# Attention loop: each output block unbroken in TensorE's queue, and the last token block's exponentials scaled in their own slot

## The chip, the cores and the metric

The kernel runs on one core of a Trainium2 chip. A core has TensorE (PE, with its weight loads, PEld), which multiplies matrices into the accumulation banks (PSUM); VectorE (DVE), ScalarE (ACT) and GpSimd (POOL), which work on elements; and SyncE (SP), from which most transfers are issued. Each engine takes its own instructions strictly in the order in which they stand in its queue, and waits at the head of the queue when an operand isn't there. The metric is the device time of one execution in microseconds (us), the median of several. For the kernel before it is 1900.26 us, over three runs from 1899.99 to 1901.23.

## The reference

Two layers of a decoder over 512 tokens of 1024 features, everything in float32. Each layer is a half-step feed-forward network, a token mixer and another half-step feed-forward network. The first mixer is a gated short convolution, the second an attention with three branches, of which the change touches two. Cut to what matters here:

```python
q = rms_norm(q) # 16 heads in 4 groups, 64 features each
s_w = q @ k_win.T * scale + rel_bias[distance]     # window branch: here every earlier token
p_w = masked_softmax(s_w, valid_w); o_w = p_w @ v_win
s_s = q @ k_sel.T * scale + rel_bias[distance]     # selected branch: here all blocks are selected
p_s = masked_softmax(s_s, valid_s); o_s = p_s @ v_sel
o_c = softmax over 31 compressed keys, times v_cmp
out = gate0 * o_c + gate1 * o_s + gate2 * o_w
return out @ w_out
```

With 512 tokens, a window of 512 and 8 blocks of which 16 may be chosen, both large branches are plain causal attention over all tokens, with different keys and values.

## The kernel before, in words

All sub-layers run one after the other, and most of the time goes to the large matrix products, which are computed with each float32 operand split in a high and a low part (`mm3`, lines 168 to 171: three matmuls each). The change lies in `attend` (from line 1200), the loop of the attention.

**Units and slots.** A unit is one head with one of the two key branches: 4 groups x 4 heads x 2 branches = 32 units. Two heads of a pair follow each other with the same branch, so units 2n and 2n + 1 share an output. The loop at line 1398 runs over slots v and is a pipeline by hand: in slot v, the scores of unit a = v + 3 are made, the exponentials of unit a - 1 are scaled, unit b = v + 1 is transposed, and in odd slots the outputs of units v - 1 and v are multiplied. Each slot has three thirds, c = 0, 1, 2, which deal with different blocks of 128 tokens: `(3,)`, then `(2, 0)`, then `(1,)` for the scores.

What each helper issues:

- `logits` (line 1271): on TensorE, two matmuls for each token block i, of the queries against the first (i + 1) x 128 keys, high and low part; 8 in a unit. The result `s` lies in one of two banks, s0 and s1, in turn.
- `smallest` (1286): on VectorE, adds the bias table, writes `L` to SBUF and keeps the smallest value of each row in `st`. This is what empties a score bank. `L` has three buffers.
- `exponentials` (1296): on ScalarE, the exponential of `L` in place, with the row's sum in `st`.
- `scaled` (1303): a reciprocal `r` of the four sums on VectorE, the factor `f` (reciprocal times gate) on GpSimd, and four in-place scalings of `L` by `f` on GpSimd, rows 0 to 3, the last of them 512 wide. It stands in the first third of the slot after the one that made the exponentials.
- `turn` (1313): ten transposes `pt` of 128 x 128 on TensorE (4, 4 and 2 in the thirds), each of which needs its row scaled, then copies `p` to SBUF, by ScalarE and (the second third) by VectorE. `pt` has three banks.
- `apply` (1329): the output block. For a pair of heads, eight float32 matmuls into one bank `o`, whose weights are 64 wide: the even head writes the lower 64 partitions, the odd head the upper 64, one after the other. The profile shows two records for each of these, so a block has 16. With the second branch two more pairs for the compressed keys follow (20 records), and the block is finished and split into `ohi` and `olo`.
- `fill` (1402): what is put in between: the query and value projections for later groups (`nat`), the output projection of finished groups (`y`), the compressed branch (`pc`, `pct`), and the turning of the next group's heads and keys (`pk`, `turned`, then moves by DMA into `q` and `k`). `nat`, `y`, `pc` and `pk` share two banks.

At each change of group, around slots 3 to 5, 11 to 13 and 19 to 21, the next group's queries and keys are normed, transposed and moved. The first scores of the new group (unit 8, 16 or 24) need them.

**What sets the order.** The order of each engine's queue is fixed when the kernel is compiled. A scheduler takes instructions in the order in which they are traced, but lets a later one go ahead when, by its estimate of the times, an earlier one isn't ready. `tc.issue_after(ins)` adds an edge for what is traced within it: on the engine of `ins`, and only there, these instructions stand behind `ins`. It adds an order in the queue, no wait. Before the change there are two such edges: `apply` stands behind the last transpose traced so far (line 1416), and the filler of the last third behind the last matmul of `apply` (line 1424). All else may fall in between the matmuls of a block, and in five of the 16 blocks it does.

## Time and profile before

| | us |
|---|---|
| median of three runs | 1900.26 |
| the profiled execution's own time | 1900.41 |
| its span, first to last instruction | 1898.6 |
| TensorE busy over the span | 1871.1 |
| VectorE busy | 1561.7 |
| ScalarE busy | 855.5 |
| GpSimd busy | 226.4 |
| stage of the attention loop | 1325 to 1533 |

Outside the span lie 1.8 us of the profiled execution. Busy time of TensorE runs from the start of a matmul to its modelled end, so that one which could overlap the next but doesn't counts as busy too; what a piece of the queue really takes is read from the starts of the instructions, or from the busy time of one tile in a window. In the views of instructions in order of time, the first number is the start in us from the span's start, the second the length, then engine, line, operation, tiles written and read, the shape, and how many are merged in the row; a number in brackets is the idle time of the engine before, with what ended it. The granted TensorE clock is 1.000 throughout.

### The profile page before, as it was taken

The page shows a single profiled execution, that of the slowest core. Times are in us where ns is not written, and L with a number is a line of the kernel's source. Part 1 is how long each engine was busy: PE and PEld are TensorE (multiplying, and loading weights), DVE is VectorE, ACT ScalarE, POOL GpSimd, SP SyncE. Part 2 cuts the span into 40 slices and gives each one's busy share as a digit, 9 for nine tenths or more (in the row PEclk, how much of TensorE's full clock was granted, in tenths as well). Part 3 has the DMA queues.
Part 4 walks back from the last instruction along what each step waited for, and adds up shares of the span by engine and source line. Part 5 has one row for each costly group of instructions (what it writes and reads, how often), then busy time and mean ns, then how long its engine had stood idle before and what let it go on. Part 6 is the DMA issues. An engine that isn't in the chain of part 4 may idle for free.

```text
span 1898.6 us, 33944 instructions
## 1 busy us (share of the span) xinstructions
PE 1871.1 (99%) x13293; PEld 1710.1 (90%) x13293; DVE 1561.7 (82%) x2671; ACT 855.5 (45%) x1399; POOL 226.4 (12%) x330
## 2 busy tenths in 40 slices
PE   6999999999999999999999999999999999999999
PEld 4989999988899899999989899999777789898989
DVE  8978888887898888888888888887778778586865
ACT  3434344532245343435634343463667636353432
POOL 0011110000011111100111110000444410010100
PEclk9999999999999999999999999999999999999999
DMA  9587767366756767664667766234333235464731
GB/s 327 177 255 191 242 181 230 116 229 233 249 156 183 233 177 239 184 218 117 172 222 189 225 176 203 82 114 127 96 90 84 70 86 160 133 189 124 187 110 64
DMA packets 126669, 324.60 MB, mean 171 GB/s; under 512 B 16011, under 2 KB 16651, under 8 KB 126508
## 3 DMA queue, kind: packets, MB, share of 16 engines
q1 hardware_dynamic: 95196, 242.72, 38.1%
q0 software_dynamic: 31312, 79.71, 18.4%
q8 instruction: 104, 1.70, 0.4%
q14 instruction: 57, 0.47, 0.1%
HBM read 313.85 MB, written 3.15 MB: 167 GB/s over the span
## 4 chain that ended last, share of the span: by engine, by line
PE 84%; DVE 8%; issue 3%; ACT 2%; POOL 1%; DMA 1%; DVEq 0%; SPq 0%; ACTq 0%; POOLq 0%
PE gu L171 13%; PE gu L169 13%; PE gu L170 13%; PE y L169 7%; PE y L170 7%; PE y L171 7%; PE cv L169 2%; PE cv L170 2%; PE cv L171 2%; PE hs L170 2%; PE hs L169 2%; PE hs L171 2%; PE ty L170 1%; PE ty L171 1%; PE o L1340 1%
## 5 line engine op out<-in xcount | busy, mean ns | idle before, releaser
L165 ACT ACTIVATE whi<-wraw 128x1024 fp32r<-128x1024 f32 (+2 forms) x261 | 254.4, 978 | 372.7 <-PE y L170 193.4
L166 DVE TENSOR_TENSOR wlo<-wraw,whi 128x1024 fp32r<-128x1024 f32 (+2 forms) x261 | 294.4, 1133 | 24.4 <-ACT whi L165 23.4
L169 PE MATMUL y<-ahi,whi 128*128 128x512 f32 x576 | 223.7, 391 | 1.0
L170 PE MATMUL y<-alo,whi 128*128 128x512 f32 x576 | 224.3, 389 | 0.0
L171 PE MATMUL y<-ahi,wlo 128*128 128x512 f32 x576 | 224.1, 389 | 0.0
L149 DVE CUSTOM_DVE_ANT_0 adaraw<-adaraw,cond,adabs 128x1024 f32<-128x1024 f32 x144 | 185.8, 1307 | 31.3 <-DMA adaraw<-in_adaw 31.0
L169 PE MATMUL gu<-hhi,whi 128*128 128x256 f32 x696 | 192.5, 277 | 0.0
L171 PE MATMUL gu<-hhi,wlo 128*128 128x256 f32 x696 | 192.4, 276 | 0.0
L170 PE MATMUL gu<-hlo,whi 128*128 128x256 f32 x696 | 192.4, 276 | 0.0
L657 POOL DMA_DIRECT2D qa<-in_ffi x70 | 84.4, 1206 | 712.9 <-DMA qa<-in_ffi 169.4
L169 PE MATMUL gu<-th,qah 128*128 128x256 f32 x584 | 161.3, 276 | 0.0
L170 PE MATMUL gu<-tl,qah 128*128 128x256 f32 x584 | 161.2, 276 | 0.0
L171 PE MATMUL gu<-th,qal 128*128 128x256 f32 x584 | 161.2, 276 | 0.0
L169 PE MATMUL gu<-th,qbh 128*128 128x256 f32 x584 | 161.2, 276 | 0.0
L170 PE MATMUL gu<-tl,qbh 128*128 128x256 f32 x584 | 161.2, 276 | 0.0
L171 PE MATMUL gu<-th,qbl 128*128 128x256 f32 x584 | 161.2, 276 | 0.0
L169 PEld LDWEIGHTS y<-ahi,whi 128*128 128x128 f32 x576 | 107.3, 188 | 27.0 <-ACT ahi L165 5.7
L169 PEld LDWEIGHTS gu<-hhi,whi 128*128 128x128 f32 x696 | 130.7, 188 | 0.5
L170 PEld LDWEIGHTS gu<-hlo,whi 128*128 128x128 f32 x696 | 130.6, 188 | 0.5
L171 PEld LDWEIGHTS gu<-hhi,wlo 128*128 128x128 f32 x696 | 130.7, 188 | 0.0
L171 PEld LDWEIGHTS y<-ahi,wlo 128*128 128x128 f32 x576 | 108.2, 188 | 22.6
L170 PEld LDWEIGHTS y<-alo,whi 128*128 128x128 f32 x576 | 108.1, 188 | 22.1
(312 smaller groups left out, 5379.8 us busy)
## 6 DMA issues: line engine op xcount, KB each, us to landing
wraw<-in_ffi SPq DMA_DIRECT2D x103, 512.0 KB
adaraw<-in_adaw POOLq DMA_DIRECT2D x79, 512.0 KB, 4.9
qa<-in_ffi SPq DMA_DIRECT2D x146, 256.0 KB
wraw<-in_ffo SPq DMA_DIRECT2D x96, 384.0 KB
qa<-in_ffi POOLq DMA_DIRECT2D x70, 512.0 KB, 6.8
adaraw<-in_adaw SPq DMA_DIRECT2D x65, 512.0 KB
a<-in_ffi SPq DMA_DIRECT2D x73, 256.0 KB
wraw<-in_cwi SPq DMA_DIRECT2D x24, 512.0 KB
```

The source lines that it names most:

```text
L149: return nc.vector.tensor_tensor_reduce(out=raw, in0=raw, in1=cond, scale=scale, scalar=adabs[:, c:c + 1], op0=ALU.mult, op1=ALU.add, accu ...
L165: act = nc.scalar.activation(hi, src, AF.Copy)
L166: return act, nc.vector.tensor_tensor(lo, src, hi, ALU.subtract)
L169: nc.tensor.matmul(o, sh, mh, start=first, stop=False)
L170: nc.tensor.matmul(o, sh, ml, start=False, stop=False)
L171: nc.tensor.matmul(o, sl, mh, start=False, stop=last)
L657: nc.gpsimd.dma_start(qa, bass.AP(tensor=a21.tensor, offset=a21.offset, ap=[a21.ap[0], [0, 2], a21.ap[1]]), accum_op=ALU.add)
L1340: last = nc.tensor.matmul(o[half[e], j * P:T], vn[b][j][:, g], both[e][0][:, cc:cc + n], start=(b == 0 and j == 0), stop=False)
```

## The change

Three things change in the loop. `scaled` takes the rows to work on: rows 0, 1 and 2 are scaled where all four were, and row 3 (the last 128 tokens), whose exponentials are made in the first third of a slot, in the last third of that same slot, so that each unit has two reciprocals and two factors, of three rows and of one. `apply` is traced within `behind_all`: an edge to each of the last 40 TensorE instructions among the last 200 instructions traced, in place of the one to the last transpose. And `logits`, `turn` and `fill` are, in every third, traced within `behind_block`, an edge to the last matmul of the newest `apply`.

```diff
-            def scaled(u):
+            def scaled(u, rows):
                 g, q, b = units[u]
+                m = slice(rows[0], rows[-1] + 1)
                 r = sp.tile([P, NB], F32, name="r")
-                nc.vector.reciprocal(r, sts[u][:, NB:2 * NB])
+                nc.vector.reciprocal(r[:, m], sts[u][:, NB + m.start:NB + m.stop])
                 f = sp.tile([P, NB], F32, name="f")
-                nc.gpsimd.tensor_tensor(f, r, gsb[:, :, (g * 4 + q) * 3 + 2 - b], ALU.mult)
-                for i in range(NB):
+                nc.gpsimd.tensor_tensor(f[:, m], r[:, m], gsb[:, m, (g * 4 + q) * 3 + 2 - b], ALU.mult)
+                for i in rows:
                     l = Ls[u][:, LOFF[i]:LOFF[i] + (i + 1) * P]
                     nc.gpsimd.tensor_scalar(l, l, f[:, i:i + 1], 0.0, op0=ALU.mult, op1=ALU.add)
...
+            @contextmanager
+            def behind_all(engine):
+                with ExitStack() as es:
+                    for i in [i for i in nc.cur_bb.bb.instructions[-200:] if i.engine == engine][-40:]:
+                        es.enter_context(tc.issue_after(i))
+                    yield
+
+            def behind_block():
+                return tc.issue_after(last_out[0].ins) if last_out else nullcontext()
+
...
                 for c in range(3):
                     if 0 <= a < N:
-                        sps = logits(a, c)
+                        with behind_block():
+                            sps = logits(a, c)
                     if c == 0 and 0 <= a - 1 < N:
-                        scaled(a - 1)
+                        scaled(a - 1, (0, 1, 2))
+                    if c == 2 and 0 <= a < N:
+                        scaled(a, (3,))
                     if 0 <= b < N:
-                        low = turn(b, c)
+                        with behind_block():
+                            low = turn(b, c)
                     if u % 2 and 0 < u and c == 2:
-                        with tc.issue_after(last_turn[0].ins):
+                        with behind_all(last_turn[0].ins.engine):
                             last_out[:] = [apply(u - 1)]
...
-                    with tc.issue_after(last_out[0].ins) if last_out and c == 2 else nullcontext():
+                    with behind_block():
                         fill(c)
```

## The prediction

> **What bounds the kernel now.** I read the page first, then the busy time of the engines over the attention stage, then that of single tiles and the instructions in order of time around the blocks that the change touches.

> ```profile
> span 1898.6 us, 33944 instructions
> PE 1871.1 (99%) x13293; PEld 1710.1 (90%) x13293; DVE 1561.7 (82%) x2671; ACT 855.5 (45%) x1399; POOL 226.4 (12%) x330
> ```
> ```profile
> 1325.00:1533.00 208.00, 203.23 (x1370) 155.75 (x1369) 160.36 (x480) 133.63 (x369) 82.05 (x160) 1.00 0.30 82
> ```

> TensorE (PE) is busy for 99% of the span, and for 203.23 of the 208 us from 1325 to 1533, which hold the loop that is changed (the columns are PE, weight loads, VectorE, ScalarE, GpSimd, then TensorE's granted clock). So TensorE's queue sets the time, what it saves or loses in this stage reaches the end almost whole (the stages behind it are matmuls again), and no engine but VectorE, 77% busy here, comes near. But a busy TensorE is not one that does its work at the best price. The output blocks show that. `apply` makes 16 of them, one for each odd slot v from 1 to 31: 16 matmul records for the first key branch, 20 for the second. Eleven stand in one piece. Of the windows below, all for tile `o` on TensorE, the first five hold the blocks that stand in pieces (slots 3, 5, 13, 21, 23), the last two a whole block of each size.

> ```profile
> 1355.70:1361.90 6.20, 4.23 (x20) 1.00 0.33 128
> 1369.20:1375.02 5.82, 3.80 (x16) 1.00 0.50 117
> 1417.80:1424.29 6.49, 3.59 (x16) 1.00 0.46 105
> 1468.00:1475.51 7.51, 3.58 (x16) 1.00 0.44 105
> 1484.10:1489.70 5.60, 4.01 (x20) 1.00 0.22 89
> 1398.80:1401.20 2.40, 2.32 (x16) 1.00 0.45 106
> 1386.20:1389.40 3.20, 3.17 (x20) 1.00 0.04 10
> ```

> A matmul of the block fills half of the array's columns (its weights are 64 wide), and its partner the other half. Held together, the two halves run side by side; where the queue is cut between partners, each runs alone.

> **The change, part by part.** *Whole blocks.* The five split ones cost 4.23 - 3.17 = 1.06, 3.80 - 2.32 = 1.48, 1.27, 1.26 and 4.01 - 3.17 = 0.84 us too much: 5.9 us in all. That is the most that holding them together can save, give or take a tenth of a microsecond at each of the ten cuts. It isn't all won, since the pieces now fill time in which TensorE would otherwise stand. Slot 5, in order:

> ```profile
> 1368.48 0.82 PE L1320 MATMUL pt<-ident,L 128*128 128x128 f32 x6
> 1369.23 1.07 PE L1340 MATMUL o<-p,vn 128*64 128x512 f32 x2
> 1370.23 0.66 PE L1166 MATMUL pk<-ident,qn 128*128 128x128 f32 x4
> 1371.82 1.25 PE L1281 MATMUL s<-k,q 128*128 128x512 f32 x6
> 1374.01 0.50 PE L1281 MATMUL s<-k,q 128*128 128x256 f32 x2
> 1375.02 0.38 PE L169 MATMUL nat<-whi,hhi 128*128 128x256 f32 x1
> ```
> ```profile
> 1368.80 0.76 DVE L1184 SCALAR_TENSOR_TENSOR k<-pk,kgs,turned 64x512 fp32r<-64x512 f32 x1
> 1370.68 1.21 DVE L166 TENSOR_TENSOR wlo<-wraw,whi 128x1024 fp32r<-128x1024 f32 x1
> 1371.93 0.74 DVE L1193 SCALAR_TENSOR_TENSOR q<-pk,qgs,turned 64x512 fp32r<-64x512 f32 x1
> 1372.87 0.69 DVE L1291 CUSTOM_DVE_ANT_0 L<-s,tb 128x512 f32<-128x512 f32 x1 [0.19 <-POOL L L1311]
> ```

> With `behind_all` the block goes behind everything of its slot: the turned heads (pk) and all three sets of scores (s). pk needs the bank that VectorE empties with `k`, until 1368.80 + 0.76 = 1369.56, so TensorE stands 0.3 us from 1369.23. The six score matmuls follow at about 1370.1 if the moved keys have landed (they have by 1371.82; no view tells how much sooner). The last two scores need one of two score banks back, which VectorE empties with the first `L`. Ahead of that in its queue is `wlo`, to 1371.89; then L takes 0.69, to 1372.6. Those scores (0.50 at 1374.01) and the block, 2.32, end at 1375.4, against 1375.02 now. If `q` stays ahead of L too, it is 1376.1; if L goes first, 1374.4. I take 0.2 lost, between 1.1 lost and 0.6 won.

> ```profile
> 1417.81 1.07 PE L1340 MATMUL o<-p,vn 128*64 128x512 f32 x2
> 1419.40 1.07 PE L1340 MATMUL o<-p,vn 128*64 128x512 f32 x4
> 1420.40 0.68 PE L1281 MATMUL s<-k,q 128*128 128x512 f32 x2
> 1422.41 0.50 PE L1281 MATMUL s<-k,q 128*128 128x256 f32 x2 [0.30 <-DVE st L1291]
> 1424.29 0.38 PE L169 MATMUL nat<-whi,hhi 128*128 128x256 f32 x1
> 1470.68 1.33 DVE L166 TENSOR_TENSOR ehlo<-wraw,ehhi 128x1024 fp32r<-128x1024 f32 x1
> ```

> Slot 13 has the same shape without a `wlo` in the way. Without the two pieces ahead of them (1.07 us each) the first scores start 1.5 to 2 us before 1420.40, at 1418.7; the last come 2.0 us later (1422.41 - 1420.40, bound by VectorE, as the 0.30 shows), and with 0.50 and 2.32 the block ends at 1423.5: 0.8 won, between 0.3 and 1.1. Slot 21 is as slot 5, with `ehlo` (1.33) in `wlo`'s place, but has six matmuls of the output projection for a filler: 0.3 won, between 0.6 lost and 0.8 won.

> ```profile
> 1357.66 0.69 DVE L1291 CUSTOM_DVE_ANT_0 L<-s,tb 128x512 f32<-128x512 f32 x1
> 1361.90 0.50 PE L1281 MATMUL s<-k,q 128*128 128x512 f32 x1
> ```

> Slot 3 is bound by the score banks. As VectorE's queue stands, its last scores can't go before the L that ends at 1357.66 + 0.69 = 1358.35; with 0.50 for them and 3.17 for the block that makes 1362.0, where the next scores stand now (1361.90): nothing, within half a microsecond.

> ```profile
> 1484.17 1.72 PE L1340 MATMUL o<-p,vn 128*64 128x512 f32 x6
> 1485.82 0.50 PE L169 MATMUL y<-ohi,whi 128*128 128x512 f32 x1
> 1487.40 0.97 PE L1340 MATMUL o<-p,vn 128*64 128x384 f32 x7
> 1489.70 0.50 PE L169 MATMUL y<-ohi,whi 128*128 128x512 f32 x1
> 1485.14 0.27 DVE L1242 TENSOR_TENSOR lc<-pc,lc 128x120 f32<-128x120 f32 x1
> ```

> In slot 23 the six y between the pieces are traced a slot earlier (the share of `out_steps(1)` puts them in slot 22), so the block must go behind them, and they wait for a bank that VectorE empties with `lc`, until 1485.41. y from 1485.5 (1.58 us, 1485.82 to 1487.40), then 3.17: 1490.3, which is 0.6 lost; if VectorE takes `lc` sooner, up to 0.84 won. I take 0.3 lost, nearer the row as it stands.

> Sum: -0.2 + 0.8 + 0.3 + 0 - 0.3 = 0.6 us won; by the ends, from 2.5 lost to 3.8 won. The eleven whole blocks and `behind_block` on the first two thirds of a slot order nothing that isn't so ordered now. Behind a waiting block stand the next slot's scores, transposes and fillers, and for them ScalarE and VectorE; only TensorE's instructions get the edge, so weights are fetched as before.

> *The last tokens' row sooner.*

> ```profile
> L1306 DVE RECIPROCAL r<-st 128x4 f32<-128x4 f32 x32 | 5.5, 172 | 4.6 <-ACT L L1300 4.3
> L1308 POOL TENSOR_TENSOR f<-r,gsb 128x4 f32<-128x4 f32 x32 | 8.6, 267 | 123.8 <-DVE r L1306 100.7 <-ACT p L1326 10.3 <-PE pt L1320 7.5
> L1311 POOL TENSOR_SCALAR L<-L,f 128x512 f32<-128x512 f32 x32 | 24.7, 773 | 0.0
> ```
> ```profile
> PEld pt L1320 <- POOL L L1311: 1.5, 4, 0.5
> PE pt L1320 <- POOL L L1311: 0.7, 2, 0.3
> ```
> ```profile
> 1364.11 2.05 POOL L1311 TENSOR_SCALAR L<-L,f 128x128 f32<-128x128 f32 x4
> 1370.42 3.05 POOL L1311 TENSOR_SCALAR L<-L,f 128x128 f32<-128x128 f32 x4
> ```

> The 512-wide scaling, 0.77 us of GpSimd, leaves the end of the chain exponentials, reciprocal, factor, scaling, transposes. TensorE waits on that chain for at most 1.5 + 0.7 = 2.2 us in the whole stage, so 2.2 is the most it gains, less what is next late. Added are 32 reciprocals (32 x 0.172 = 5.5 us of VectorE) and 32 factors (32 x 0.267 = 8.5 us of GpSimd). GpSimd, 82 of 208 us busy, hides its own. VectorE has 48 us free, but hardly any around the three changes of group (slots 3 to 5 and their like), where each extra reciprocal of two or three units delays the L on which the scores wait: up to 3 x 3 x 0.172 = 1.5 us lost. The new reciprocal waits for exponentials made two thirds of a slot earlier, so what is queued behind it on VectorE (smallest, the copy of p) seldom stands. I take 0.5 won, between 1.5 lost and 2.2 won. The two GpSimd rows are the same four scalings and factors of the same unit kind, once 2.05 and once 3.05 us; in the second VectorE's `wlo` (1370.68, 1.21 us, two SBUF inputs) ran beside it. [...]

> Both parts: 0.6 + 0.5 = 1.1 us won. The profiled run took 1900.41 us, 0.15 above the median of the three, 1900.26, so the forecast is 1899.3 there and 1899.2 for the median; by the ends (4.0 lost, 6.0 won) 1894.3 to 1904.3. A measurement of this kernel can tell about 0.2%, 3.8 us, from no change.

> **The rivals.** *The whole saving lands.* The stage's order is computed when the kernel is compiled, and with the pieces gone it may put L ahead of `wlo`, `q` and `lc`. Then the holes close and 5.9 of the blocks and a little of the scaling arrive: 1900.3 - 6.3 = 1894.0. For it: VectorE's 48 free us, and at 1420.40 nothing but order holds the scores. Against it: the rows of slots 3 and 5, where VectorE works without a break.

> *The score banks turn over too slowly.* Two banks hold the scores, and each waits for VectorE's L. Now pieces of the block run while it does so; afterwards nothing may. If at each change of group the keys arrive only at 1371.82 and L stays where it is, at 1372.87, the last scores of slot 5 go at 1373.6 (1372.87 + 0.69) and the block ends 0.50 + 2.32 later, at 1376.4: 1.4 lost, three times, and 0.6 in slot 23. That is 4.8 lost: 1905.1. It decides once a change of group loses more than about 1.1 us.

> *The edges don't hold the blocks.* `behind_all` takes the last 40 of TensorE's instructions among the last 200 traced; what is older could still fall in between, and the time stays at 1900 within a microsecond. The y of slot 23, the oldest that I know, stands only 22 back on TensorE by the code (a slot makes 8 score matmuls and 10 transposes, and y falls after the second third), so this is unlikely.

> **How the numbers follow.** Forecast 0.50, whole saving 0.27, slow banks 0.18, blocks not held 0.05. By itself the likeliest case spans 1896 to 1903. Faster by over 0.2% (under 1896.5): the whole saving and a tail of the forecast, 0.30. Slower by over 0.2% (over 1904.1): the slow banks, 0.18. Within: 0.52. The range, 1893.0 to 1905.2, takes in the two rivals about their centres and leaves a tenth at each end.

> **What would show it.** Tile `o` should take 2.32 or 3.17 us in each of 16 unbroken blocks, so that the five windows lose 5.9 us together. If the forecast holds, most of that comes back as TensorE waiting for VectorE's `st`, `k` or `lc` just before slots 3, 5, 21 and 23. r and f should count 64 each, and the 2.2 us of waiting for GpSimd fall below 1. I am wrong if the stage from 1325 to the last block shrinks by over 4 us, or grows; and if the time moves outside this stage.

## The result, and the profile after

The kernel after takes 1924.36 us (median of 4 runs, 1923.69 to 1926.27); the kernel before, run beside it, 1900.74 us (1899.99 to 1902.09). The ratio is 1.0128, 95% interval 1.0113 to 1.0143: 24 us slower, 19 us beyond the upper end of the range, and on the side that had the smallest chance.

From the page of the kernel after, the span, the busy time of the engines and the granted clock in 40 slices:

```profile
span 1921.9 us, 34093 instructions
...
PE 1875.0 (98%) x13293; PEld 1713.5 (89%) x13293; DVE 1566.3 (81%) x2703; ACT 858.2 (45%) x1399; POOL 234.2 (12%) x362
...
PE   7999999999999999999999999999788999999999
...
PEclk9999999999999999999999999999899999999999
```

The span grew by 23.3 us (1921.9 - 1898.6). TensorE does the same 13293 matmuls and is only 3.9 us busier, so most of the time is idle. And the slices show where: the 29th to the 31st (48.05 us each, so 1345 to 1490 us) have 7, 8 and 8 tenths of TensorE, and the first of them a granted clock of 8 tenths, where the page of before has a 9 in all of these. In the shares of the whole span, 99% against 98%, 23 us hardly show.

The windows of the output blocks, tile `o` on TensorE in the kernel after (length, busy time and records, granted clock, DMA share, GB/s):

```profile
1353.90:1357.80 3.90, 3.64 (x16) 0.66 0.82 334
1369.80:1375.00 5.20, 5.06 (x20) 0.63 0.36 76
1424.80:1429.80 5.00, 4.87 (x20) 0.66 0.37 79
1481.40:1487.20 5.80, 5.56 (x20) 0.58 0.29 65
1384.00:1387.00 3.00, 2.37 (x16) 1.00 0.35 79
1397.00:1401.00 4.00, 3.23 (x20) 1.00 0.02 4
```

All 16 blocks now stand in one piece, as the change wants, and twelve take 2.37 or 3.23 us in this view (the last two rows). The other four, those of slots 1, 3, 11 and 19, have a granted clock of about 0.6 beside them and take 1.27 + 1.83 + 1.64 + 2.33 = 7.1 us more than the short ones. Three of them (slots 1, 11 and 19) were whole before, and cost nothing then.

The chain of waits on TensorE from 1325 to 1560, after (total us, times, longest), and the same view of before:

```profile
PE pk L1166 <- DVE qn L960: 14.5, 3, 5.6
PE pct L1262 <- DVE pcs L1257: 6.7, 1, 6.7
PE s L1281 <- DVE st L1291: 2.8, 4, 1.2
```
```profile
PE s L1281 <- DVE st L1291: 1.7, 5, 0.5
PE pt L1320 <- POOL L L1311: 0.7, 2, 0.3
PE pk L1166 <- DVE qn L960: 0.6, 2, 0.4
```

Four waits make 21.2 us: one for the compressed probabilities `pcs`, ahead of their transposes `pct`, and three for the normed heads `qn`, ahead of their transposes `pk`. Before, the two together cost 0.6. In order of time around slot 3, before and then after:

```profile
1359.19 0.48 PE L1281 MATMUL s<-k,q 128*128 128x256 f32 x2
1359.61 0.97 PE L1340 MATMUL o<-p,vn 128*64 128x384 f32 x7
...
1360.79 1.19 PE L1345 MATMUL o<-pcp,vz 128*64 128x512 f32 x3
...
1362.48 0.60 PE L1320 MATMUL pt<-ident,L 128*128 128x128 f32 x4
1362.91 0.38 PE L1166 MATMUL pk<-ident,kn 128*128 128x128 f32 x2
1363.13 0.38 PE L1166 MATMUL pk<-ident,qn 128*128 128x128 f32 x2
```
```profile
1363.85 0.38 PE L1321 MATMUL pt<-ident,L 128*128 128x128 f32 x2
1368.67 1.29 PE L1166 MATMUL pk<-ident,qn 128*128 128x128 f32 x4 [4.45 <-DVE qn L960]
1369.90 4.20 PE L1341 MATMUL o<-p,vn 128*64 128x512 f32 x16
1373.93 1.02 PE L1346 MATMUL o<-pcp,vz 128*64 128x512 f32 x4
1374.89 0.74 PE L1281 MATMUL s<-k,q 128*128 128x512 f32 x2
```

Before, the block and the next scores go first, and the first pk that reads `qn` follows 3.5 us after the slot's last scores (1363.13 against 1359.19 + 0.48 = 1359.67), without a wait. After, this pk goes first. VectorE makes `qn` no sooner: from the reduction of `vq` to the end of `qn` it takes 8.9 us (from 1360.31), against 8.5 before (from 1354.51). So TensorE stands for 4.45 us (such a stretch is called a hole below); behind pk stands the block, whose operands were turned in earlier slots, and behind the block all of the next slot. The row of VectorE that makes `qn` before, then VectorE in the hole, after:

```profile
1361.75 1.29 DVE L960 TENSOR_TENSOR qn<-qn,rs_r 128x512 f32<-128x512 f32 x2
```

```profile
1363.44 1.22 DVE L166 TENSOR_TENSOR wlo<-wraw,whi 128x1024 fp32r<-128x1024 f32 x1
...
1366.18 0.47 DVE L216 TENSOR_TENSOR rs_a<-rs_r 128x16 f32<-128x16 f32 x1
...
1367.34 0.56 DVE L220 SCALAR_TENSOR_TENSOR rs_r<-rs_a,rs_r 128x16 f32<-128x16 f32 x1
1367.93 1.29 DVE L960 TENSOR_TENSOR qn<-qn,rs_r 128x512 f32<-128x512 f32 x2
```

It works its way through the inverse square root of the norms, small steps between scores and copies, and reaches `qn` at 1367.93.

The same instructions that follow a hole are slow. Four pk records take 1.29 us here; the prediction's row of before has 0.66 for four. The clock over this stretch, after (the columns of the engines as in the prediction):

```profile
1366.80:1373.60 6.80, 4.92 (x18) 2.25 (x20) 3.94 (x11) 1.29 (x3) 2.48 (x6) 0.50 0.37 102
1364.00:1366.70 2.70, 0.23 (x3) 0.00 (x0) 2.70 (x13) 2.62 (x10) 1.62 (x4) 1.00 0.35 79
```

The granted clock is 1.00 for the first 2.6 us of the hole (which starts at 1364.22) and 0.50 for the 6.8 us after that, well into the block. The holes of slots 1, 11 and 19 show the same: one spell at 0.50 each, of 6.8 us, begun 3.5, 2.2 and 4.8 us into the hole. The clock is 1.00 in every other block. The trace shows no one length of standing as the condition: the spells begin 2.2 to 4.8 us into holes of 4.45 to 6.72 us, and the two holes of 4.45 us (slots 3 and 11) differ in it by 0.4 us. Their beginnings are 1349.74, 1366.80, 1421.42 and 1479.44, worked out from the mean clock of 0.69, 0.52, 0.58 and 0.72 in the windows of 0.1 us from 1349.70, 1366.80, 1421.40 and 1479.40: the later three lie 17.06, 71.68 and 129.70 us behind the first. To within 0.1 us that is 5, 21 and 38 times half a spell (6.83 / 2; the one of slot 3 ends at 1373.63, by 0.84 in the window from 1373.60). So the length of a hole doesn't by itself tell when its spell begins.

So the sum: 21.2 us of waits, less 0.6 of before; 7.1 us in the four blocks; pct (1.09 us for four in the order of time, against 0.66) and three sets of pk (1.29 each, against 0.66) 2.3 more; less the 5.9 us of the split blocks that are whole now: 24.1, against 23.3 of the span.

### The profile page after: what moved, and what is told of

It reads as the page before. It is cut to its first block, busy times and chain, and to the rows that moved or that the text cites. A ratio compares the mean times of both kernels' runs of the same rounds, so it can differ in the third digit from the quotient of the medians.

```text
span 1921.9 us, 34093 instructions
## 1 busy us (share of the span) xinstructions
PE 1875.0 (98%) x13293; PEld 1713.5 (89%) x13293; DVE 1566.3 (81%) x2703; ACT 858.2 (45%) x1399; POOL 234.2 (12%) x362
## 4 chain that ended last, share of the span: by engine, by line
PE 89%; DVE 7%; ACT 2%; issue 1%; DMA 1%; DVEq 0%; SPq 0%; ACTq 0%
PE gu L171 13%; PE gu L169 13%; PE gu L170 13%; PE y L169 7%; PE y L171 7%; PE y L170 7%; PE o L1341 2%; PE cv L169 2%; PE cv L170 2%; PE cv L171 2%; PE hs L170 2%; PE hs L169 2%; PE hs L171 2%; PE ty L170 2%; PE ty L171 2%; PE ty L169 2%
## 5 line engine op out<-in xcount | busy, mean ns | idle before, releaser
L166 DVE TENSOR_TENSOR wlo<-wraw,whi 128x1024 fp32r<-128x1024 f32 (+2 forms) x261 | 293.8, 1131 | 24.0 <-ACT whi L165 22.8
L169 PE MATMUL y<-ahi,whi 128*128 128x512 f32 x576 | 223.7, 392 | 1.0
L169 PE MATMUL gu<-hhi,whi 128*128 128x256 f32 x696 | 192.5, 277 | 0.0
L169 PE MATMUL gu<-th,qah 128*128 128x256 f32 x584 | 161.4, 276 | 0.0
L169 PE MATMUL gu<-th,qbh 128*128 128x256 f32 x584 | 161.2, 276 | 0.0
L169 PEld LDWEIGHTS y<-ahi,whi 128*128 128x128 f32 x576 | 107.3, 188 | 26.9 <-ACT ahi L165 5.6
L169 PEld LDWEIGHTS gu<-hhi,whi 128*128 128x128 f32 x696 | 130.6, 188 | 0.5
```

Source lines behind the costliest of these rows:

```text
L166: return act, nc.vector.tensor_tensor(lo, src, hi, ALU.subtract)
L169: nc.tensor.matmul(o, sh, mh, start=first, stop=False)
```

## The experiments

The theory: `pct` (slot 0's last third) and the first half of the next group's heads, `pk` (the second third of slots 3, 11 and 19), are traced ahead of the blocks of slots 1, 3, 11 and 19, and they wait for VectorE. `behind_all` puts the block behind them; `behind_block` puts everything later behind the block. Together the edges leave nothing that TensorE may do in the wait, and a long wait (4.45 us and more in this kernel) is followed by half the clock (0.50). The rivals: the scaled row delays VectorE; one edge alone costs the time; whole blocks cost it; or the score banks do.

**The scaled part alone** (before, with only this, and `scaled` taking rows as in the change):

```diff
-                        scaled(a - 1)
+                        scaled(a - 1, (0, 1, 2))
+                    if c == 2 and 0 <= a < N:
+                        scaled(a, (3,))
```

> The kernel before with the split of the scaling alone (row 3 in its own slot, rows 0 to 2 a slot later); no new edges in TensorE's queue. Theory (the block is queued behind fillers that wait for VectorE): no hole, 1900.7 us within 3. Rival A (the extra reciprocals and factors delay the chain of exponentials): most of the 24 us is here, 1912 us or more, with TensorE waiting for GpSimd or for L. Rival B (what is held behind the block starves VectorE and ScalarE): 1900.7 within 3.

1900.06 us, ratio 0.9999 (0.9990 to 1.0008). It does nothing, to within 2 us. The whole loss lies with the edges.

**`behind_all` alone** (before, with only this):

```diff
-                        with tc.issue_after(last_turn[0].ins):
+                        with behind_all(last_turn[0].ins.engine):
```

> The kernel before with one edit: the output block stands behind the last 40 TensorE instructions. All four rows are scaled together, and nothing new is held behind the block. Theory: four holes of 4 to 7 us, before pct in slot 1 and before pk in slots 3, 11 and 19, each followed by some 7 us at half clock: 1918 to 1928 us. Rival A: 1900 within 4. Rival B: 1900 within 4, since scores and transposes may go on during a hole.

1902.99 us, ratio 1.0015 (1.0005 to 1.0024). This missed: I had put the whole loss on this edge, and it is 3 us. TensorE's waits and the block of slot 3:

```profile
PE pk L1166 <- DVE qn L960: 5.9, 5, 3.5
```
```profile
1365.14 1.04 PE L1166 MATMUL pk<-ident,qn 128*128 128x128 f32 x6 [3.48 <-DVE qn L960]
1366.11 4.04 PE L1341 MATMUL o<-p,vn 128*64 128x512 f32 x16
```

All blocks are whole and stand behind pct and pk, as in the kernel after. But the next slot's scores and transposes aren't tied to the block, and go ahead of it while pct and pk wait: 5.9 us of waiting for `qn` instead of 14.5, and none for `pcs` in this view. Where the wait is still 3.48 us, the block behind it takes 4.85 us (1366.11 to the next matmul at 1370.96), at a granted clock of 0.67 from 1365.80 to 1371.00. The block of slot 11 is slow too: it runs from 1417.20 to 1422.12, 4.92 us, at a lower clock (0.74 in the window below), though the longest wait ahead of it is 1.27 us:

```profile
1416.23 0.44 PE L1166 MATMUL pk<-ident,qn 128*128 128x128 f32 x2 [1.27 <-DVE qn L960]
```
```profile
1417.50:1424.00 6.50, 4.62 (x20) 0.74 0.50 114
```

So the 3 us are a difference: 5.3 us more waiting for `qn` and 3.3 more in these two blocks, less the 5.9 of the blocks that are whole now.

**`behind_block` alone** (before, with only the edge on `logits`, `turn` and `fill`; the first two are put within `behind_block()` as in the change, of the third this is the edit):

```diff
-                    with tc.issue_after(last_out[0].ins) if last_out and c == 2 else nullcontext():
+                    with behind_block():
                         fill(c)
```

> The kernel before with one edit: scores, transposes and fillers of every third stand behind the newest block, while the block itself stands only behind the last transpose. Theory: no hole over 2 us, no half clock, 1897 to 1904 us. Rival A: 1900 within 2. Rival B: 1912 us or more, with VectorE waiting for scores.

1899.67 us, ratio 0.9998 (0.9989 to 1.0008). Nothing, and the blocks stay in pieces. So alone the edges are worth about 3 us and 0, and together 24: the loss is in what they do together.

**Both edges, without the scaled part** (after, with all four rows scaled in one place).

```diff
-                        scaled(a - 1, (0, 1, 2))
-                    if c == 2 and 0 <= a < N:
-                        scaled(a, (3,))
+                        scaled(a - 1, (0, 1, 2, 3))
```

> The change without its scaled part: all four token blocks of the scaling stand in one slot as before, both edges (block behind the instructions ahead of it; later scores, turns and fillers behind the block) are kept. Theory (the two edges together close the queue around a block that waits for VectorE): the loss is theirs alone, so 1922 to 1926 us, and the four holes ahead of pct (once) and pk (three times) sum to 19 to 23 us. Rival (the early scaling of the last tokens delays VectorE's norm chain, since POOL and VectorE then work at the same time, and the holes are longer for it): a part of the loss goes, 1910 to 1920 us.

1922.47 us, ratio 1.0118 (1.0103 to 1.0133); the waits for `qn` and `pcs` are 13.1 and 6.7 us. The edges alone make the loss.

**The block behind its own slot's scores and transposes only** (after; fillers traced ahead no longer hold it; `ahead_` collects the score matmuls and transposes, 8 and 10 in a slot):

```diff
-                    for i in [i for i in nc.cur_bb.bb.instructions[-200:] if i.engine == engine][-40:]:
-                        es.enter_context(tc.issue_after(i))
+                    for i in ahead_[-18:]:
+                        es.enter_context(tc.issue_after(i.ins))
```

> The changed kernel, but the block stands behind the 8 score matmuls and 10 transposes of its slot alone, not behind pct, pk, nat, pc or y. Theory: the four holes and the half clock go, and most blocks stay whole; 1893 to 1901 us. Rival A: 1915 us or more, the scaling being as in the changed kernel. Rival B: 1915 us or more, the rest being held behind the block as in the changed kernel.

1899.05 us, ratio 0.9995 (0.9986 to 1.0004). 25 us are back, with the blocks whole but for slot 23's, which is cut once by a `y`. Whole blocks don't cost the time; the fillers ahead of them do.

**One hole put back** (the run above, with slot 3's block alone behind all 40):

```diff
-                    for i in ahead_[-18:]:
-                        es.enter_context(tc.issue_after(i.ins))
+                    for i in [i for i in nc.cur_bb.bb.instructions[-200:] if i.engine == engine][-40:] if v == 3 else [i.ins for i in ahead_[-18:]]:
+                        es.enter_context(tc.issue_after(i))
```

> The kernel of the run without the filler ahead (every block behind only its slot's scores and transposes, 1899.05 us), with the block of slot 3 alone put behind all forty instructions, pk of heads among them. Theory: one hole of 4 to 5 us ahead of that pk, half clock behind it, worth 1.8 us on the block and 0.8 us on pk; together 6 to 8 us: 1905 to 1907 us. If holes cost no more than their own idle time: 1903 to 1904 us. If the four holes only cost by what they do to one another (VectorE later from slot to slot): within 2 us of 1899.

1904.76 us, ratio 1.0026 (1.0016 to 1.0035): 5.7 us for one hole, a little under what I expected. Slot 3, in order of time, and the window of its block:

```profile
1361.44 0.44 PE L1166 MATMUL pk<-ident,qn 128*128 128x128 f32 x2 [3.81 <-DVE qn L960]
1362.04 0.65 PE L1166 MATMUL pk<-ident,qn 128*128 128x128 f32 x2 [0.17 <-DVE qn L960]
1362.61 3.81 PE L1342 MATMUL o<-p,vn 128*64 128x512 f32 x16
```
```profile
1362.50:1367.30 4.80, 4.67 (x20) 0.68 0.34 78
```

The hole is 3.81 us (0.24 in the run without it) and the block takes 4.67 instead of 3.23. Together that is 5.0 us. It can't be set against the 5.7 to the microsecond: the two profiled executions differ by 3.9 us (1903.24 and 1899.38), the medians by 5.7. No other slot's edges were touched, so a hole doesn't need the others to cost this much.

**Idle work in the holes** (after, with 24 matmuls of 128 x 128, identity by identity, ahead of the four waiting fillers; their result is read by nothing). The run asks whether the blocks behind the holes are slow because of the lower clock (0.58 to 0.66 in their windows), and whether it stays away when TensorE doesn't stand:

```diff
+            def idle_work(n):
+                o = psum("dm", "t")
+                for _ in range(n):
+                    nc.tensor.matmul(o[:, 0:P], ident, ident, start=True, stop=True)
+            for v, c in ((0, 2), (3, 1), (11, 1), (19, 1)):
+                places[v, c].insert(0, lambda: idle_work(24))
```

> The change with its whole diff, and 24 added matmuls of 128x128 (identity by identity, into a bank of their own that nothing reads) traced ahead of the waiting fillers of slots 0, 3, 11 and 19, so that TensorE is not idle for all of a hole. [...] Rival (the blocks behind a hole are slow for another reason, such as operands that arrive late, and the lower clock only goes with it): the blocks stay at 4.8 us or more and the time is 1924 us or more.

1920.01 us, ratio 1.0110 (1.0093 to 1.0127). The groups of the added work and of pk, and the window of the stretch around slot 3:

```profile
L1412 PE MATMUL dm<-ident 128*128 128x128 f32 x192 | 22.4, 276 | 0.0
L1166 PE MATMUL pk<-ident,qn 128*128 128x128 f32 x24 | 4.4, 285 | 1.2 <-DVE qn L960 0.6 <-DVE k L1184 0.5
```
```profile
1362.00:1373.50 11.50, 11.36 (x89) 8.94 (x88) 8.51 (x29) 5.91 (x16) 5.81 (x12) 1.00 0.28 76
```

In the profiled execution TensorE does 22.4 us of useless work in place of 21.2 us of standing, the clock is 1.00 throughout (0.998 to 0.999 on average in the other three), every block takes its short time again, and tile `o` falls from 51.90 us to 44.85 between 1325 and 1556:

```profile
1325.00:1556.00 231.00, 51.90 (x288) 0.94 0.28 73
```
```profile
1325.00:1556.00 231.00, 44.85 (x288) 1.00 0.28 79
```

The rival (the blocks are slow for another reason) is out by these block times. The gain in time is less sure: 4.4 us by the medians and 3.4 by the two ratios, whose intervals overlap. The total stands 1 us above the 1912 to 1919 us that I expected if the clock stayed at 1.00: by the medians, of the 7.1 us won on the blocks and 2 on pk and pct, 1.2 go to the added work being longer than the holes, and the waits for VectorE elsewhere (3.8 us for `st` against 2.8, and a `y` that waits 1.6) grew; the remaining 0.9 us isn't accounted for.

**The waiting fillers traced behind the block** (after, otherwise whole; the two edits move these fillers in every group):

```diff
-                    places[v0 - 5, 1].append(lambda g=g: heads(g, 0))
+                    places[v0 - 5, 2].append(lambda g=g: heads(g, 0))
...
-                for place in ((v0 - 2, 0), (v0 - 2, 1), (v0 - 1, 0), (v0 - 1, 1), (v0 - 1, 2), (v0, 2)):
+                for place in ((v0 - 2, 0), (v0 - 2, 1), (v0 - 1, 0), (v0 - 1, 1), (v0 - 1, 2), (v0 + 1, 2)):
```

> The change with its whole diff, but the two waiting fillers are traced behind the block: the first half of heads moves from the second third to the last third of its slot, and the last compressed step (pct) from the last third of slot 0 to that of slot 1. Theory (pct and pk stand ahead of the block and hold it): the block no longer waits for them, the four holes go, no half clock is left, and the time is 1893 to 1901 us. Rival (every block that is held behind forty instructions and holds all behind it loses, whatever the filler): 1915 us or more. A third outcome: the fillers wait as long at their new place, now behind the block with 3.2 us of cover: pk still waits 1 to 3 us each time, 1901 to 1910 us.

1898.24 us, ratio 0.9992 (0.9982 to 1.0001). The whole change stands, with both edges, and 26 us are back by two positions in the trace. All 16 blocks are whole, at a granted clock of 1.000, and pk waits 0.8 us in all. Tile `o` takes 44.85 us against 50.83 before, 6.0 less; yet the kernel gains only some 1.5, and the interval takes in no change at all. Where the rest went, by groups on TensorE (the last column is idle time ahead of the group, and what ended it):

```profile
L1281 PE MATMUL s<-k,q 128*128 128x512 f32 (+3 forms) x256 | 60.2, 337 | 2.6 <-DVE st L1291 2.4
L1321 PE MATMUL pt<-ident,L 128*128 128x128 f32 x320 | 51.6, 276 | 1.1 <-DVE p L1326 0.6 <-POOL L L1312 0.2
L169 PE MATMUL y<-ohi,whi 128*128 128x512 f32 x32 | 13.9, 436 | 1.7 <-ACT p L1327 0.8 <-DVE k L1184 0.4 <-DVE lc L1242 0.4
```

These waits come mostly from VectorE. Two more kernels tell whether VectorE holds the rest.

**The same, with one scaling per unit** (the split scaling taken out of the run above):

> The kernel with the waiting fillers traced behind the block (1898.24 us, 0.9992), with the four token blocks scaled together as before the change. The split scaling issues a second reciprocal of 0.16 us on VectorE for each of 32 units, 5.2 us in all. Theory A (what the whole blocks win, 5.3 us, is given back as waits for VectorE, for the score banks above all): less work on VectorE lets a part through, 1896 to 1898 us, and the idle time of s<-k,q falls below 2.6 us. Theory B (the split scaling is neutral here too, as it was alone): within 0.7 us of 1898.2.

1896.94 us, ratio 0.9984 (0.9975 to 0.9993). Within the first theory's range in time, but its 3.2 us of waiting for `st` didn't fall, and the two intervals overlap. Not decided by this run.

**And eight copies moved from VectorE to ScalarE** (the run above, with this; tried also on the kernel before, without edges):

```diff
-                if c == 1:
+                if c == 1 and u not in (1, 2, 3, 4, 11, 12, 19, 20):
                     return lambda: nc.vector.tensor_copy(p, pt[:, 0:off])
```

> As the run above, and in the eight slots in which or ahead of which VectorE carries the norms of heads and the compressed steps (0 to 3, 10, 11, 18, 19) the copy of 512 turned columns, 0.68 us on VectorE, is made by ScalarE. Theory A (VectorE holds the score banks in these slots): the waits for the score banks, 2.4 us in six places before, fall to under 1.2 us, and the time is 1.5 to 3 us below the run above, under both kernels. Theory B (ScalarE's exponentials, in the same slots, come later by as much, or the waits have another cause): within 1 us of the run above, or above it.

> The kernel before, with nothing of the change, and the eight copies of 512 turned columns on ScalarE as in the run above (1893.53 us, 0.9966). If the copies help wherever VectorE is late, and the whole blocks' share is the 2.9 us of the run with fillers behind the block and one scaling, the copies alone are worth 2.5 to 4 us: 1896 to 1897.5 us. If they help only where whole blocks have made VectorE the one that is late (the kernel before waits 1.7 us for the score banks in all): 1898.5 to 1900 us.

With whole blocks: 1893.53 us, ratio 0.9966 (0.9952 to 0.9980). On the kernel before, alone: 1900.52 us, ratio 1.0004 (0.9995 to 1.0014). The same eight copies are worth 3.4 us with the edges and nothing without them. VectorE from 1345 to 1375 (third number in the row) with whole blocks, without the copies moved and then with them:

```profile
1345.00:1375.00 30.00, 27.35 (x189) 19.58 (x188) 28.91 (x84) 22.04 (x58) 13.20 (x24) 1.00 0.38 88
```
```profile
1345.00:1375.00 30.00, 29.11 (x209) 21.69 (x208) 25.20 (x79) 23.30 (x64) 11.72 (x25) 1.00 0.36 77
```

VectorE was busy 28.91 of 30 us there; with 3.7 us less on VectorE, TensorE works 1.8 us more in the same time. That speaks for VectorE as what held this stretch. But it was nearly as busy in the kernel before (28.18 us in the same window), and the copies shortened TensorE's standing there too: from 1325 to 1533 it is busy for 205.08 us with them and for 203.23 without, 1.9 us less standing, and its waits for `st` fell from 1.7 to 0.8 us. What took that back is in tile `o`, in the kernel before with the copies moved:

```profile
1325.00:1556.00 231.00, 53.87 (x288) 1.00 0.31 82
```

That is 3.0 us more than the 50.83 of before: without the edges, the order that was compiled anew cuts the blocks into more pieces, those of slots 11 and 19 among them, which had been whole. So the copies save waiting in both kernels, and the edges keep the gain by keeping the blocks whole. That whole blocks had first made VectorE the engine that is late isn't shown. One sign was not as expected: the waits for `st` fell only from 3.2 to 2.4 us, not under 1.2; what went besides were those for `k` (1.0 us to none) and for the scaled rows (0.7 to none). This version beats both kernels, by 0.34% and some 1.6%.

## Why the prediction was wrong

- **That TensorE's queue sets the time** held, more than it was used: 21 us of standing there reached the end almost whole.
- **The five split blocks, 5.9 us**, held. With every block whole and no hole, tile `o` takes 6.0 us less.
- **That most of it is given back** held in the run in which the block is tied to nothing but its slot's own matmuls: 1.0 us won there (1899.05 against 1900.06, no change within the interval), 0.6 forecast for this part. That a lighter VectorE at the changes of group then wins 3.4 us speaks for VectorE as the taker; how it divides among the waits is not shown.
- **The scaled row**: 0.5 taken, between 1.5 lost and 2.2 won; measured 0.0, within 2 us. The size was small enough not to matter. The wait of TensorE for the scaled rows fell to nothing in the kernel after, as expected, without being of use.
- **The step that failed** is the sentence "The eleven whole blocks and `behind_block` on the first two thirds of a slot order nothing that isn't so ordered now". It looked at a block as a thing that stands in one piece or not. That it stands in one piece doesn't say what stands ahead of it. The blocks of slots 1, 11 and 19 were whole in the kernel before and ran ahead of pct and pk, which are traced earlier; so `behind_all` turned their order around, and `behind_block` took away what else could have gone. In the kernel before, for slots 1 and 11 (slot 19 is the same, with the block at 1458.11 and pk at 1462.76):

```profile
1347.37 2.37 PE L1340 MATMUL o<-p,vn 128*64 128x512 f32 x16
...
1354.64 0.66 PE L1262 MATMUL pct<-ident,pcs 128*128 128x128 f32 x4
...
1407.91 2.37 PE L1340 MATMUL o<-p,vn 128*64 128x512 f32 x16
...
1412.21 0.44 PE L1166 MATMUL pk<-ident,qn 128*128 128x128 f32 x2 [0.18 <-DVE qn L960]
```

What the runs showed in place of the nothing that the sentence assumes is 21.2 us of standing ahead of four blocks. Three of the four holes came from blocks that the prediction had counted as untouched. The fourth is slot 3, where "bound by the score banks" left out the heads that are traced ahead of its block: pk could not go before `qn`, which VectorE ended at 1363.04 (1361.75 + 1.29), 3.4 us after the slot's last scores, and the block had been the cover. By the rows of before that makes 1363.04 + 0.66 for pk + 3.17 for the block = 1366.9 against 1361.90, 5.0 us lost where the prediction has nothing within half a microsecond; the run with one hole lost 5.7.
- **The clock** was in no term. The prediction took the price of a wait as its length. A long one costs more: 7.1 us on four blocks and 2.3 us on pk and pct, a good third of the loss.
- **The rival on the slow side** had the sign, and one piece of the mechanism (afterwards nothing may run in the wait), but put it at the score banks, with 4.8 us. Waiting for the score banks grew by 1.1 us, from 1.7 to 2.8.

## What to carry to other kernels

Before tying a block to all that is traced ahead of it, list for each of its places which instructions ahead the scheduler had let it overtake, and when their operands come; the time from the last unblocked instruction to that operand is the hole, and a second edge that ties the later work to the block takes away what would fill it. Trace an instruction that waits for another engine behind the block that covers the wait, not ahead. And when an edit does nothing, see whether it saved waiting and the order compiled anew spent it elsewhere (here 1.9 us less standing and 3.0 us more in cut blocks): with the order held, the same edit can be worth its time.

## What the runs showed of the hardware

Output blocks of 64-wide matmuls, 16 records each, took 2.37 us whole, and up to 3.80 us where others were put in between. Two records cut off from their partners took 1.07 us (before, from 1417.81), as long as four that stood together (from 1419.40).
